# An encoder layer with RWKV-7 time mixing: the chain step on the full array, products that cross between token halves, and projections by halves

## The chip, the cores and the metric

The kernel runs on one core of a Trainium2 chip. The metric is the device time of one execution in microseconds (us). Three runs of the kernel before took 1292.1, 1293.94 and 1299.46 us, median 1293.94.

## The reference

One layer of a streaming encoder works on 576 tokens: 64 that continue a running stream and 512 of a new one. The model is 1024 wide. With h the normalised input, one wide projection feeds three parts, and a gated feed-forward follows:

```python
h = rms_norm(x, g_pre_mix); p = h @ w_in     # r, k, v, three low-rank inputs | u, v of the gMLP | two gates
# time mixing: 16 heads of 64; per token, per head, with decay w, a = -kk, b = kk * a_rate:
sa = einsum('bhvk,bhk->bhv', S, a)
S  = S * w + sa[..., None] * b[:, :, None, :] + v[..., None] * k[:, :, None, :]
y  = einsum('bhvk,bhk->bhv', S, r)
o_a = (group_norm(y) + bonus) * g
o_b = u * (tril(w_spatial) @ layer_norm(v) + bias)            # per chunk of 128 tokens
m = sigmoid(gate_a) * (o_a @ w_proj_a) + sigmoid(gate_b) * (o_b @ w_proj_b)
x = x + rms_norm(m @ w_o); x = x + rms_norm((silu(f @ w_gate) * (f @ w_up)) @ w_down)   # f = rms_norm(x)
```

`r`, `k` and `v` are first mixed with the token before them (token shift). All is fp32. Outputs are the layer's output, the last shifted rows, the final states of both streams and the normalised gMLP rows.

## The kernel before, in words

*Layout.* Activations stand transposed, 128 channels on the partitions and T = 576 tokens along a row (64 of the running stream first), in eight tiles. `HALF` is 288 tokens. A weight block of 128 output columns is one DMA of 512 KB (`wraw`) and is split into a high part `whi` (ScalarE, L289) and a low part `wlo` (GpSimd, two pieces, L292) of the type fp32r; the input likewise into `h0h..h7h` and `h0l..h7l`. A product of a block is then three fp32r products for each of eight k tiles and each token half (`mm`): 48 instructions of 288 columns, `pj` in the profile.

*PSUM.* Eight banks of 512 columns: two tiles of two banks for projections (`ps2`; a projection lies across both banks, columns 224 to 799), three single banks for small products (`ps1`), one for the chain (`ps1c`).

*Time mixing.* The 16 heads are worked as eight pairs (two heads of 64 on the 128 partitions), the tokens as nine chunks of 64. For each pair:

- `elementwise`: decay and rates (`z` products), sums over heads (`n`), the scaled operands `AR` (a and r) and `BK` (b and k); inner products of 64 x 64 within a chunk (`am`), masked into `AB` and `AK`; transposes of b, a, k, v into by-token tiles `Bt`, `At`, `Kt`, `Vt` (`tb`, `tr`, `tv`); `WV`; and the bonus (`bo`).
- `inverse`: the unit triangular 64 x 64 matrix of each chunk and head is inverted: 16 x 16 blocks go through DRAM (`d_inv`) onto 80 partitions, are inverted by 30 VectorE operations (`X`, `Xt`), come back, and are put together by products `m1`, `m2`, `mp`, `mu` into `IT`. `IT` times `Bt` and times the second half of `AB` are the `d` products; `e` are the transition terms (`At` with the result), `c` the constant terms; `y` the part of the output that needs no state.
- `chain`: the state goes from chunk to chunk: `pc` is the transition matrix times the state, VectorE adds the constant term `C` (L916). Chunk 0 is the running stream, chunks 1 to 8 the new one. `py` adds the state's part to `y`.
- `finish`: group norm, transposes back (`to`), gate (`g`).

By-token tiles hold five places of 128 tokens, starting at tokens 0, 128, 256, 384 and 448 (`START`); a place has two halves of 64 partitions (`HR`), so each chunk lies in one half. A product of 64 x 64 uses one of four tiles of TensorE's array: the input's half of partitions by the output's.

*What sets the order.* TensorE's order is written by a planner (`Weave`), when the program is built: streams of small products, each step with an event or a planned latency (`LAT`) before it, are woven into the projections; whenever no stream is ready, the next piece of a projection follows (`project`, one k tile and one half a piece). The planner's clock `clk.now` advances by an estimate for each product. `F0` and `FILL` say how many blocks of gates and u are put between the pairs. The other engines' orders come from the framework's scheduler. In both versions every engine works through its own order and waits on semaphores.

*After the pairs* come the gMLP projections (`gv`), both output projections (`pa`, `pb`), `w_o` (`po`), the feed-forward (`fp`, `fg`) and `w_down` (`po`).

## Time and profile before

| | us |
|---|---|
| median of three runs | 1293.94 |
| the profiled execution, its own time | 1290.25 |
| its span, first to last instruction | 1288.2 |
| of it, TensorE busy | 1218.9 |
| first 60 us, TensorE busy | 44.9 |
| 60 to 630 (the eight pairs and gMLP projections), TensorE busy | 537.0 |
| 630 to 697 (layer norm, first output products), TensorE busy | 59.3 |
| 697 to the end, TensorE busy | 577.7 |

In a row of the timeline the first number is the start, the second the time to the end of the last of its instructions, both in us. Products overlap, so the difference of two starts tells what one costs in a sequence; "busy" is the union of their modelled spans. `PE` is TensorE, `DVE` VectorE, `ACT` ScalarE, `POOL` GpSimd, `SP` the queue that issues DMAs. A row of waits gives the total, the number and the longest. The mean granted TensorE clock of this execution is 0.977 of full speed.

### The profile page before, as it was taken

The numbers are of one execution on the slowest core, as the hardware profiler recorded it, in microseconds if no ns is written. First come the engines' busy times: TensorE is split into PE (matmuls) and PEld (weight loads), VectorE is DVE, ScalarE is ACT, GpSimd is POOL, SyncE is SP. The second block draws the span as 40 slices with busy tenths as digits, with TensorE's granted clock in tenths as the row PEclk, the third lists the DMA queues.
The fourth block names the chain that finished last, engine by engine and source line by source line (L and its number), as shares of the span: only waits on it lengthen the run. The fifth ranks groups of instructions, "written<-read, shape, count | busy, mean of one in ns | idle before, by whom it ended". The sixth has DMA issues, their size and how long they took to land.

```text
span 1288.2 us, 30705 instructions
## 1 busy us (share of the span) xinstructions
PE 1218.9 (95%) x13402; PEld 1171.4 (91%) x13402; DVE 561.4 (44%) x1001; ACT 454.9 (35%) x800; POOL 632.0 (49%) x491
## 2 busy tenths in 40 slices
PE   7799999999999889899989999989999999999997
PEld 6798898888889888889979999989999999999997
DVE  5864645554554636562481443274333333310013
ACT  5634352535253343433332223453222222222220
POOL 6564463442444444431484544356656565644342
PEclk8899999899899999999999999989999999999998
DMA  5222132222131322222535454232222222252222
GB/s 177 79 84 74 47 90 64 69 57 87 41 104 52 89 69 49 81 73 79 168 124 154 136 177 128 69 114 82 94 82 82 83 83 83 82 164 74 84 81 74
DMA packets 68406, 118.61 MB, mean 92 GB/s; under 512 B 30832, under 2 KB 36208, under 8 KB 68272
## 3 DMA queue, kind: packets, MB, share of 16 engines
q1 hardware_dynamic: 68128, 116.58, 30.0%
q8 instruction: 105, 1.72, 0.6%
q14 instruction: 29, 0.24, 0.1%
q10 hardware_dynamic: 144, 0.07, 0.0%
HBM read 100.35 MB, written 16.28 MB: 91 GB/s over the span
## 4 chain that ended last, share of the span: by engine, by line
PE 71%; DVE 13%; ACT 4%; issue 4%; DMA 4%; POOL 2%; SPq 2%; DVEq 0%; ACTq 0%; POOLq 0%
PE fg L273 20%; PE po L273 14%; PE pj L273 13%; PE pb L273 4%; PE pa L273 3%; PE gv L273 3%; DVE Xt L794 2%; DVE X L797 2%; PE am L273 2%; PE y L273 2%; PE d L273 1%; SPq L802 1%; PE fp L273 1%; PE z L273 1%; POOL wlo L292 1%
## 5 line engine op out<-in xcount | busy, mean ns | idle before, releaser
L292 POOL TENSOR_TENSOR wlo<-raw,whi 128x512 fp32r<-128x512 f32 (+1 forms) x288 | 407.3, 1436 | 358.8 <-ACT whi L289 342.4
L289 ACT ACTIVATE whi<-raw 128x1024 fp32r<-128x1024 f32 x144 | 149.8, 1044 | 282.0 <-PE fg L273 172.8
L1179 DVE TENSOR_TENSOR rs<-rs,nsq 128x288 f32<-128x288 f32 (+2 forms) x12 | 9.2, 768 | 104.6 <-ACT nsq L1178 104.6
L1247 DVE TENSOR_TENSOR ft<-ft,fg 128x288 f32<-128x288 f32 x40 | 16.4, 451 | 67.1 <-PE fg L273 65.5
L1241 DVE TENSOR_TENSOR fg<-fg,rs 128x288 f32<-128x288 f32 x40 | 16.5, 453 | 62.3 <-PE fg L273 62.2
L710 POOL TENSOR_TENSOR BK<-BK,EL 128x576 f32<-128x576 f32 x16 | 18.4, 1169 | 49.8 <-PE am L273 45.8
L794 DVE TENSOR_TENSOR Xt<-X,M 80x15 f32<-80x15 f32 (+7 forms) x120 | 35.2, 293 | 8.1 <-DMA M<-d_inv 4.9
L1244 DVE SCALAR_TENSOR_TENSOR ft<-ft,fg 128x576 f32<-128x576 f32 (+1 forms) x24 | 28.9, 1206 | 18.7 <-ACT ft L1243 18.7
L643 POOL TENSOR_TENSOR aq<-aq,k 128x576 f32<-128x576 f32 x8 | 11.8, 1479 | 50.9 <-DVE k L465 49.6
L797 DVE TENSOR_TENSOR X<-X,Xt 80x15 f32<-80x15 f32 (+7 forms) x120 | 35.0, 292 | 3.6
L805 DVE STREAM_TRANSPOSE IT<-IV 128x640 f32<-128x640 f32 x16 | 13.5, 844 | 52.9 <-DMA IV<-d_inv 32.1
L1245 POOL TENSOR_TENSOR ft<-ft,rs 128x576 f32<-128x576 f32 (+1 forms) x24 | 31.8, 1325 | 7.3 <-DVE ft L1244 7.3
L273 PE MATMUL pj<-h4l,whi 128*128 128x288 f32 x92 | 28.6, 311 | 5.5 <-DVE h4l L342 5.5
L273 PE MATMUL am<-AR,BK 64*64 64x128 f32 x640 | 28.5, 284 | 3.4 <-DVE AR L866 1.8
L916 DVE TENSOR_TENSOR S<-pc,C 128x64 f32<-128x64 f32 x48 | 10.7, 222 | 48.3 <-PE pc L273 48.0
L273 PE MATMUL pj<-h0h,whi 128*128 128x288 f32 x92 | 28.7, 312 | 2.7 <-ACT s L431 1.4
L273 PE MATMUL pj<-h0h,wlo 128*128 128x288 f32 x92 | 27.6, 300 | 3.7 <-POOL wlo L292 3.7
L273 PE MATMUL pj<-h5h,whi 128*128 128x288 f32 x92 | 30.3, 329 | 0.0
L273 PE MATMUL pj<-h4h,whi 128*128 128x288 f32 x92 | 29.8, 324 | 0.0
L273 PE MATMUL pj<-h6h,whi 128*128 128x288 f32 x92 | 29.7, 323 | 0.0
L273 PE MATMUL pj<-h3h,whi 128*128 128x288 f32 x92 | 29.3, 319 | 0.0
L273 PE MATMUL pj<-h2h,whi 128*128 128x288 f32 x92 | 29.2, 318 | 0.0
(1239 smaller groups left out, 4331.3 us busy)
## 6 DMA issues: line engine op xcount, KB each, us to landing
raw<-in_w_in SPq DMA_DIRECT2D x50, 512.0 KB, 3.7
raw<-in_w_gate SPq DMA_DIRECT2D x22, 512.0 KB, 3.6
raw<-in_w_up SPq DMA_DIRECT2D x22, 512.0 KB, 3.6
raw<-in_w_down SPq DMA_DIRECT2D x16, 512.0 KB, 3.5
raw<-in_w_gv SPq DMA_DIRECT2D x8, 512.0 KB, 3.7
raw<-in_w_proj_a SPq DMA_DIRECT2D x8, 512.0 KB, 3.7
raw<-in_w_proj_b SPq DMA_DIRECT2D x8, 512.0 KB, 3.5
raw<-in_w_o SPq DMA_DIRECT2D x8, 512.0 KB, 3.5
```

What stands on the lines that cost most here:

```text
L273: return pe.matmul(out, lhsT, rhs, **kw)
L289: keep(act.activation(hi[:, :cols], raw[:, :cols], ACT.Copy))
L292: keep(pool.tensor_tensor(lo[:, c0:c1], raw[:, c0:c1], f(hi[:, c0:c1]), ALU.subtract))
L710: pool.tensor_tensor(by_chunk(BK[:, x, :]), by_chunk(BK[:, x, :]), EL[:, :, 64:65].broadcast_to([P, NCH, 64]), ALU.mult)
L794: ins = dve.tensor_tensor(t3, X[:, 0:r, s:s + 1].broadcast_to([NU, r, w]), M[:, s:s + 1, s + 1:SB].broadcast_to([NU, r, w]), ALU.mult)
L797: dve.tensor_tensor(X[:, 0:r, s + 1:SB], X[:, 0:r, s + 1:SB], t3, ALU.add)
L802: sp.dma_start(IV[r0_:r0_ + SB, :, SB * b:SB * b + SB], di[1, h, b].rearrange("u s t -> s u t"))
L805: turn = lambda: dve.transpose(IT.rearrange("p c t -> p (c t)"), IV.rearrange("p c t -> p (c t)"))
L1241: keep(dve.tensor_tensor(g[:, HS[h]], pg, rs2[:, HS[h]], ALU.mult))
L1244: keep(dve.scalar_tensor_tensor(t[:, ts], t[:, ts], 1.0, g[:, ts], ALU.add, ALU.mult))
L1245: pool.tensor_tensor(t[:, ts], t[:, ts], rs2[:, ts], ALU.mult)
L1247: dve.tensor_tensor(t[:, HS[h]], t[:, HS[h]], pu, ALU.mult)
```

## The change

- *Chain step.* A new tile `TD` holds, for each chunk, a 128 x 128 matrix with the two heads' transition matrices on its diagonal (cleared once). VectorE writes the two blocks from `e`, each head's half by itself. `pc` is then one product on the full array where two 64 x 64 products were.
- *Crossing products.* A second placement, `START2` = 0, 128, 192, 320, 448, holds `AB` and the by-token b, now columns 128 to 191 of `AB` (`Bt` is gone). `d` reads in this placement, writes in the first, and does both operands in one product of 128 columns; `y` reads in the first and writes in the second, and so does the transposition back. The order (`CROSS`) goes round the four tiles.
- *Larger runs.* `d`, `e` and `c` are one run each without planned latencies between the thirds of `d`; `e` waits for the event `values` and the chain of the pair before; the inner products come in two runs where three were; `y` in one where two were.
- *Projections.* Each token half has a bank of its own and is done for all eight k tiles before the other (`project`; evacuation by halves, `Shifted`, `spill`). Three banks for projections, four for small products, one for the chain.
- *Planner.* 0.12 us for a change of the tile's rows, other costs of small products, new latencies.

```diff
...
-    "M": 5.5, "U": 18.5, "m1": 1.8, "m2": 1.7, "mp": 3.3, "mu": 2.0, "d0": 2.2, "d": 0.5, "e0": 1.5, "e1": 0.4, "y0": 1.0,
-    "ch0": 3.0, "S": 1.6, "y": 0.5, "gn1": 4.0, "gn2": 6.0, "to": 3.5, "to1": 0.45, "g": 1.8,
+    "M": 5.5, "U": 20.0, "m1": 2.3, "m2": 2.4, "mp": 3.3, "mu": 2.0, "d0": 2.2, "e0": 2.3, "y0": 3.5,
+    "ch0": 2.6, "S": 1.5, "y": 0.5, "gn1": 4.0, "gn2": 6.0, "to": 3.5, "to1": 0.45, "g": 1.8,
...
-    nb = {"d": 2, "a": 3}
+    nb = {"a": 4}
...
-    ps2 = lambda name: psum.tile([P, 1024], F32, tag="d", bufs=nb["d"], name=name)
+    psd = lambda name: psum.tile([P, 512], F32, tag="d", bufs=3, name=name)
...
+        if rows != clk.rows:
+            clk.now += 0.12
+            clk.rows = rows
...
-            ps = ps2("pj")
-            for k in range(KD):
-                for h in range(2):
-                    mm(ps, ws, hh, hl, k, KD, halves=(h,))
+            held = []
+            for h in range(2):
+                ps = psd("pj")[:, 0:HALF]
+                for k in range(KD):
+                    mm({h: ps}, ws, hh, hl, k, KD, halves=(h,))
                     yield
-            while after is not None and after not in clk.events:
-                yield True
-            done(ps)
+                held.append((h, ps))
+                while h == 1 and after is not None and after not in clk.events:
+                    yield True
+                while held and (after is None or after in clk.events):
+                    done(*held.pop(0))
...
+    class Shifted:
+
+
+        def __init__(self, blk, tag, tp=None, scale=False):
+            self.blk, self.tag, self.tp, self.scale = blk, tag, tp, scale
+
+        def __call__(self, h, ps):
+            blk, hs = self.blk, HS[h]
+            if h == 0:
+                tp = ep if self.tp is None else self.tp
+                self.o = tp.tile([P, T], F32, tag=self.tag, name=self.tag)
+                self.q = tp.tile([P, T + 1], F32, tag="q", name="q")
+            o, q = self.o, self.q
+            if self.scale:
                 dve.tensor_tensor(o[:, hs], ps, rs0[:, hs], ALU.mult)
...
+                ps = o[:, hs]
+            e = (TS, HALF)[h]
+            act.activation(shc[:, blk, h:h + 1], ps[:, e - 1:e], ACT.Copy)
+            act.activation(q[:, hs.start + 1:hs.stop + 1], ps, ACT.Copy, scale=V("mu", blk))
+            if h == 0:
+                act.activation(q[:, 0:TS + 1:TS], first[:, blk, :], ACT.Copy)
+            with tc.high_priority(HPO):
+                dve.scalar_tensor_tensor(o[:, hs], ps, omm[:, blk:blk + 1], q[:, hs], ALU.mult, ALU.add)
+            return o
...
+        for h in range(4):
+            if h == 2:
+                wr = wblock(I["w_in"][BLK_R])
...
+            for k in range(2 if h == 0 else 0, KD):
+                mm(ps, w, uh, ul, k, KD, halves=(h % 2,))
+            if h == 3:
                 clk.prepare()
...
+            act.activation(kr[-1][:, HS[h % 2]], ps[0], ACT.Copy)
...
+    START, START2 = [min(j * P, T - P) for j in range(5)], [0, 128, 192, 320, 448]
+    PLACES, PLACES2 = [[(st[j] // 64 + half_, j, half_) for j in range(5) for half_ in range(2)] for st in (START, START2)]
     CHUNKS = [(c, j, half_) for c, j, half_ in PLACES if (j, half_) != (4, 0)]
     PLACE = {c: (j, half_) for c, j, half_ in CHUNKS}
+    PLACE2 = {c: (j, half_) for c, j, half_ in PLACES2 if (j, half_) != (2, 0)}
+
+    CROSS = [(c, c // 4) for i in range(4) for c in ((i, 4 + i) if i % 2 == 0 else (4 + i, i))] + [(8, 2)]
...
+        pm = banks()
+        for c, j, half_ in PLACES2[:8]:
+            for h, rows in enumerate(HR):
+                inner(pm[h][:, j], HR[half_], rows, 0, c)
+        pn = banks()
+        for c, j, half_ in PLACES2[8:]:
             for x in range(2):
                 for h, rows in enumerate(HR):
-                    inner(pm[h][:, x], HR[half_], rows, x, c)
+                    inner(pn[h][:, x], HR[half_], rows, x, c)
         for h in range(2):
...
+            dve.tensor_tensor(AB[:, 0:4, h, 0:P], pm[h], rmul[:, 0:4, h, :], ALU.mult)
+        for h in range(2):
+            dve.tensor_tensor(AB[:, 4, h, 0:P], pn[h][:, 0], rmul[:, 4, h, :], ALU.mult)
...
-        for i, (dst, src) in enumerate(((Bt, BK[:, 0, :]), (At, AR[:, 0, :]), (Kt, BK[:, 1, :]))):
+        for i, (dst, src) in enumerate(((AB, BK[:, 0, :]), (At, AR[:, 0, :]), (Kt, BK[:, 1, :]))):
             pt = ps1("tb").rearrange("p (j v) -> p j v", v=P)
             for j in range(5):
-                mtrans(pt[:, j] if j < 4 else rest[:, i], src[:, START[j]:START[j] + P], ident)
+                t0 = (START, START2)[i == 0][j]
...
+                    dve.tensor_tensor(dst.rearrange("p j h t -> p (j h) t")[:, u, P:], ps.rearrange("p j (h v) -> p (j h) v", v=HD), rn[:, u].unsqueeze(2).broadcast_to([P, 2 * (j1 - j0), HD]), ALU.mult)
...
-        Bt, At, Kt, Vt, AR, AK, WV = (E[n] for n in ("Bt", "At", "Kt", "Vt", "AR", "AK", "WV"))
-        Bu = Bt.rearrange("p j (h v) -> p (j h) v", v=HD)
-        for u0, u1 in ((0, 4), (4, 8), (8, 10)):
-            pp = ps1("d").rearrange("p (u t) -> p u t", t=P)
-            for u in range(u0, u1):
-                for rows in HR:
-                    mmul(pp[rows, u - u0, 0:64], IT[rows, u, :], Bu[rows, u, :], start=True, stop=True)
-                for rows in HR:
-                    mmul(pp[rows, u - u0, 64:P], IT[rows, u, :], U[rows, u, 64:P], start=True, stop=True)
-            act.activation(U[:, u0:u1], pp[:, 0:u1 - u0], ACT.Copy)
-            yield LAT["d"]
-        yield LAT["e0"]
+        At, Kt, Vt, AR, AK, WV = (E[n] for n in ("At", "Kt", "Vt", "AR", "AK", "WV"))
+        pp = [ps1("d").rearrange("p (u t) -> p u t", t=P) for _ in range(3)]
+        for c, b in CROSS:
+            (j2, half2), (j, half_) = PLACE2[c], PLACE[c]
+            for h in range(2):
+                mmul(pp[b][HR[half_], 2 * (j % 2) + h], IT[HR[half2], 2 * j2 + h, :], AB[HR[half2], j2, h, 64:192], start=True, stop=True)
+        for b, rows, j0, j1 in ((0, slice(0, P), 0, 2), (1, slice(0, P), 2, 4), (2, HR[1], 4, 5)):
+            act.activation(AB[rows, j0:j1, :, 0:P].rearrange("p j h t -> p (j h) t"), pp[b][rows, 0:2 * (j1 - j0)], ACT.Copy)
+        yield (("values", hp_), LAT["e0"])
+        if hp_ > 0:
+            yield (("chain", hp_ - 1), 0.0)
+
 
         pe_ = [ps1("e").rearrange("p (j a t) -> p j a t", a=2, t=64) for _ in range(2)]
...
+        for n in range(2):
+            for c, j, half_ in CHUNKS:
+                for h in range(2):
+                    w, x = (Kt[HR[half_], j, HR[h]], Vt[HR[half_], j, HR[h]]) if n == 0 else (AB[HR[half_], j, h, 64:P], WV[HR[half_], 2 * j + h, :])
+                    mmul(pq[half_][HR[h], j * HD:(j + 1) * HD], w, x, start=n == 0 and j == 0, stop=n == 1, skip_group_check=True)
+        pe8 = pq[1][:, 5 * HD:5 * HD + P].rearrange("p (j a t) -> p j a t", a=2, t=64)
+        for h in range(2):
+            step(pe8[:, 0], 4, 1, h, start=False, skip_group_check=True)
...
+        parts = [(pe_[0], slice(0, 8, 2)), (pe_[1], slice(1, 8, 2)), (pe8, slice(8, 9))]
+        for ps, cs in parts:
+            for rows in HR:
+                dve.tensor_tensor(TD[rows, cs, rows], ps[rows, :, 1, :], by_place[rows, cs, 0, :], ALU.add)
+            dve.tensor_tensor(by_place[:, cs, 1, :], ps[:, :, 0, :], by_place[:, cs, 1, :], ALU.add)
         for half_ in range(2):
...
+            n = 4 + half_
+            act.activation(C[:, half_, 0:n], pq[half_][:, 0:n * HD].rearrange("p (j v) -> p j v", v=HD), ACT.Copy)
         clk.signal("inv", hp_)
         yield LAT["y0"]
         Y = rp2.tile([P, 5, P], F32, tag="Y", bufs=2, name="Y")
...
-                for c, j, half_ in PLACES[2 * j0:2 * j1]:
-                    for h in range(2):
-                        rows, u = HR[half_], 2 * j + h
-                        w, x = (AK[rows, j, h, 64:P], Vt[rows, j, HR[h]]) if n == 0 else (AB[rows, j, h, 64:P], WV[rows, u, :])
-                        mmul(py[rows, u - 2 * j0], w, x, start=n == 0 and (j, h) == (j0, 0), stop=n == 1, skip_group_check=True)
...
+        py = [ps1("y").rearrange("p (u v) -> p u v", v=HD) for _ in range(3)]
+        order = [x for c, _ in CROSS for x in ([(c, *PLACE2[c])] + ([(3, 2, 0)] if c == 3 else []))]
+        for n in range(2):
+            begun = set()
+            for c, j2, half2 in order:
+                b, (j, half_) = j2 // 2, PLACE[c]
+                rows = HR[half_]
+                for h in range(2):
+                    w, x = (AK[rows, j, h, 64:P], Vt[rows, j, HR[h]]) if n == 0 else (AB[rows, j, h, 0:64], WV[rows, 2 * j + h, :])
+                    mmul(py[b][HR[half2], 2 * (j2 % 2) + h], w, x, start=n == 0 and (b, half2) not in begun, stop=n == 1, skip_group_check=True)
+                    begun.add((b, half2))
...
-        cols = lambda c: slice(c * 64, (c + 1) * 64)
         for n, cs in enumerate([(2, 0)] + [(c,) for c in range(3, NCH)]):
             pc = ps1c("pc").rearrange("p (i v) -> p i v", v=HD)
             for i, c in enumerate(cs):
-                for rows in HR:
-                    mmul(pc[rows, i], AR[rows, 0, cols(c)], state(c)[rows], start=i == 0, stop=True, skip_group_check=True)
+                mmul(pc[:, i], TD[:, c, :], state(c), start=True, stop=True)
...
```

More of the change, by code (lines that the diff above doesn't have):

```diff
@@ L143, in __init__ @@
     def __init__(self):
-        self.now = 0.0
+        self.now, self.rows = 0.0, P
         self.events = {}
@@ L271, in mmul @@
         else:
-            clk.now += max(n / 1200, 0.02)
+            clk.now += n / 2000 if rows == 64 else 0.037 if rows == 32 else 0.02
         return pe.matmul(out, lhsT, rhs, **kw)
@@ L556, in layer @@
     dve.tensor_tensor(dar[0:64], xw[64:128], f(dar[64:128]), ALU.subtract)
-    xg = shifted(BLK_DG, "v", list(zip(pf[1], HS)), tp=xp)
+    take = Shifted(BLK_DG, "v", xp, True)
+    xg = [take(h, pf[1][h]) for h in range(2)][1]
     tg = xp.tile([P, T], F32, name="tg")
```

192 lines of the change are left out of this document (74 added, 118 removed).

## The prediction

> **What bounds the kernel now.** I read the stage table first, then TensorE's timeline at single runs of small products, then TensorE's waits, then the instruction order of both kernels.
>
> ```profile
> span 1288.2 us, 30705 instructions
> 60.00:630.00 570.00, 537.00 (x8352) 496.47 (x8352) 290.98 (x609) 227.10 (x461) 238.84 (x186) 0.98 0.25 70
> 697.00:1288.20 591.20, 577.67 (x4332) 573.49 (x4330) 185.41 (x296) 168.46 (x249) 310.04 (x234) 0.99 0.33 101
> 740.52 50.77 PE pb L273 x384
> ```
>
> The last row is from the chain of waits: 384 products of 288 columns without a break in 50.77 us, 0.132 us each, the pace of a projection too. The columns of the stage rows are length, busy time of TensorE, of its weight load, of VectorE, ScalarE and GpSimd, granted clock, DMA share and GB/s. The change lies in the first 60 us and in 60 to 630, where all eight head pairs are worked; after 697 the program is the same. In the pair stage TensorE is busy 537 of 570 us, VectorE 291, ScalarE 227, GpSimd 239. So the stage ends when TensorE has issued its list, and two things matter: how long the list is, and where TensorE waits inside it.
>
> A busy share does not tell what an instruction costs there, since the small products overlap. I take the cost of a run of small products from starts: from the last projection before it to the second projection after it, less two projections at 0.132.
>
> ```profile
> 208.76 0.29 PE L273 MATMUL pj<-h1h,wlo 128*128 128x288 f32 x1
> 208.98 0.33 PE L273 MATMUL pc<-S,AR 64*64 64x64 f32 x4
> ...
> 209.49 0.29 PE L273 MATMUL pj<-h2l,whi 128*128 128x288 f32 x1
> 186.53 0.29 PE L273 MATMUL pj<-h0h,wlo 128*128 128x288 f32 x1
> 186.76 0.33 PE L273 MATMUL d<-Bt,IT 64*64 64x64 f32 x4
> ...
> 188.07 0.29 PE L273 MATMUL pj<-h1l,whi 128*128 128x288 f32 x1
> 201.38 0.29 PE L273 MATMUL pj<-h5h,wlo 128*128 128x288 f32 x1
> 201.60 1.20 PE L273 MATMUL y<-Vt,AK 64*64 64x64 f32 x32
> 202.58 1.15 PE L273 MATMUL y<-WV,AB 64*64 64x64 f32 x32
> ...
> 203.90 0.30 PE L273 MATMUL pj<-h5l,whi 128*128 128x288 f32 x1
> 130.17 0.29 PE L273 MATMUL pj<-h2h,wlo 128*128 128x288 f32 x1
> 130.39 1.10 PE L273 MATMUL e<-AB,At 64*64 64x128 f32 x32
> ...
> 131.66 0.29 PE L273 MATMUL pj<-h3l,whi 128*128 128x288 f32 x1
> ```
>
> Each program instruction on plain fp32 shows as two passes. One chain step (pc, 4 passes): 0.73 - 0.26 = 0.47 us. One third of the d products (16 products, 32 passes, of which the first group of four is shown): 1.54 - 0.26 = 1.28. y: 64 passes, 2.26. pc, d and y use only the two tiles whose input and output halves agree, so they are 2, 16 and 32 passes deep. 1.28 - 0.47 over 14 passes gives 0.058 us for a 64-column pass; what is left, 0.35 us, is paid by every run of small products however short. Check on y: 0.35 + 32 x 0.058 = 2.21 against 2.26. The e run goes over all four tiles, 8 deep: (1.23 - 0.35) / 8 = 0.11 us for a 128-column pass.
>
> So the changeover is the larger part of a chain step, and two of the four tiles stand empty in d and y.
>
> **The change, part by part.** On TensorE, around the second pair's products with the inverses, the chain kernel's order was this before (d: products with the inverse, am: inner products of the next pair, e and c: terms of the chain):
>
> ```order
> L273 MATMUL d<-Bt,IT 64x64 x2
> L273 MATMUL d<-AB,IT 64x64 x2
> L273 MATMUL am<-AR,BK 64x128 x16
> L273 MATMUL pj<-h3h,whi 128x288
> L273 MATMUL pj<-h3l,whi 128x288
> ```
>
> and is this now, in the same place:
>
> ```order
> L271 MATMUL pj<-h7h,wlo 128x288
> L271 MATMUL d<-AB,IT 64x128 x18
> L271 MATMUL e<-AB,At 64x128 x16
> L271 MATMUL c<-Vt,Kt 64x64 x18
> L271 MATMUL c<-WV,AB 64x64 x18
> L271 MATMUL c<-AB,At 64x128 x2
> L271 MATMUL am<-AR,BK 64x128 x16
> L271 MATMUL pj<-h0h,whi 128x288
> ```
>
> All of d, e and c stand in one run, in every one of the eight pairs; projections between d and e, there before, are gone. At a chain step the order was (pc the step, pj projections):
>
> ```order
> L273 MATMUL pj<-h1h,wlo 128x288
> L273 MATMUL pc<-S,AR 64x64 x2
> L273 MATMUL pj<-h2h,whi 128x288
> L273 MATMUL pj<-h2l,whi 128x288
> L273 MATMUL pj<-h2h,wlo 128x288
> ```
>
> and is
>
> ```order
> L271 MATMUL pj<-h0h,wlo 128x288
> L271 MATMUL pc<-S,TD 128x64
> L271 MATMUL pj<-h1h,whi 128x288
> L271 MATMUL pj<-h1l,whi 128x288
> L271 MATMUL pj<-h1h,wlo 128x288
> ```
>
> The step is one full-array product now. Counted over the whole order, runs of small-tile products fall from 142 to 68.
>
> *Changeovers:* 74 fewer x 0.35 = 25.9 us.
>
> *d:* before 40 passes deep a pair, 40 x 0.058 = 2.32; now 18 products of 128 columns over four tiles, the fullest with three chunks x 2 heads x 2 passes, 12 x 0.11 = 1.31. 8 x 1.01 = 8.1 us.
>
> *y:* 40 deep, 2.32, becomes 24 deep (three chunks x 2 heads x 2 terms x 2 passes on the fullest tile), 24 x 0.058 = 1.39, if four tiles of 64 columns go at once. The py products of before do that:
>
> ```profile
> 220.29 0.29 PE L273 MATMUL pj<-h0h,wlo 128*128 128x288 f32 x1
> ...
> 220.75 0.57 PE L273 MATMUL py<-S,AR 64*64 64x64 f32 x26
> 221.49 0.30 PE L273 MATMUL pj<-h1l,whi 128*128 128x288 f32 x1
> 396.15 0.29 PE L273 MATMUL pj<-h3h,wlo 128*128 128x288 f32 x1
> 396.29 1.17 PE L273 MATMUL n<-cst,q 128*128 128x2 f32 x10
> 397.53 0.29 PE L273 MATMUL pj<-h4l,whi 128*128 128x288 f32 x1
> ```
>
> 40 passes, 10 deep on four tiles, take 1.20 - 0.26 = 0.94 (0.35 + 10 x 0.058 = 0.93). So y saves 8 x 0.93 = 7.4 us.
>
> *Chain:* the trace has no full-array product of 64 fp32 columns; nearest is n, 10 passes in 1.38 - 0.26 = 1.12, 0.112 a pass, no changeover. A pair's eight products cost 8 x 2 x 0.112 = 1.79 against 16 passes of 0.058, 0.93: 8 x 0.86 = 6.9 us more (ends: 4 if half of a pass hides behind a projection; 9 at a projection's 0.13 a pass). Its changeovers are in the 74.
>
> The list is shorter by 25.9 + 8.1 + 7.4 - 6.9 = **34.5 us**.
>
> *Waits that go or stay:*
>
> ```profile
> PE m L273 <- ACT PT L816: 8.5, 5, 2.9
> PE tv L277 <- DVE Y L928: 5.1, 3, 2.1
> PE c L273 <- DVE AR L866: 2.9, 2, 1.7
> PE n L273 <- ACT q L639: 2.1, 1, 2.1
> PE am L273 <- DVE AR L866: 1.8, 3, 0.6
> PE am L273 <- ACT AB L853: 1.4, 1, 1.4
> PE c L273 <- DVE AK L688: 1.4, 2, 0.7
> ```
>
> The tv wait is for a PSUM bank that py holds. Now the small products have four banks for three, and tv stands ahead of py or far from it: 5.1 go. The four c and am waits, 7.5, are bank waits inside merged runs; they go with those runs. The m waits (the inverse) I leave as they are: ends -8.5 and +5.
>
> *Waits that come:*
>
> ```profile
> 187.97 0.58 ACT L853 ACTIVATE AB<-d 128x512 f32<-128x512 f32 x1
> 187.02 1.04 ACT L289 ACTIVATE whi<-raw 128x1024 fp32r<-128x1024 f32 x1
> L866 DVE TENSOR_TENSOR AR<-e,AR x16: 628/680/692, 131.8 to 606.6; 128x512 f32<-128x512 f32 x16
> L883 DVE TENSOR_TENSOR AR<-e,AR x8: 291/292/292, 134.2 to 608.4; 128x128 f32<-128x128 f32 x8
> ```
>
> e reads what ScalarE copies from d's banks, and nothing stands between. The copy takes 0.58 and starts about 0.3 after the last pass (d's first third ends by 187.7); first and second bank are full 4 passes (0.44) before d ends. So 0.3 + 0.58 + 0.1 - 0.44 = 0.55, and 0.15 more for the second copy: 0.7 x 8 = 5.6 us (upper end: a weight cast of 1.04 ahead of the copy each time, 14). Behind e all of TensorE's list waits. In four pairs am follows c at once and needs e's second bank, which six VectorE adds empty; 256 columns lie between the two rows above, 0.42 each: 0.3 + 2.5 - 1.3 (c) = 1.5 x 4 = 6. In four pairs d follows am or nearly so and needs the banks that VectorE empties: about 0.75 x 4 = 3. Waits together: +14.6 - 12.6 = **+2 us**.
>
> *DMAs and the other queues.* The eight stores of AB to DRAM that feed the inverse, on SP, stood behind AK's two evacuations on VectorE (L688, the size of the 0.68 row above) and now wait for AB alone: some 1.3 us earlier, in a step that TensorE's order gives more time anyway; I count nothing (cover: the projections between; without it the m waits above). Loads of weights, stores of gates and GpSimd's casts keep number and size; GpSimd clears TD once, at a place where TensorE works off projections.
>
> *Halves of projections* change neither count nor width. They add ScalarE and VectorE instructions (two where one was), hidden behind TensorE as long as it bounds. They cost at the start, where VectorE makes the input tiles:
>
> ```profile
> 45.66 0.29 PE L273 MATMUL pj<-h4h,whi 128*128 128x288 f32 x1
> 51.45 0.61 PE L273 MATMUL pj<-h4l,whi 128*128 128x288 f32 x1 [5.50 <-DVE h4l L342]
> 49.57 1.82 DVE L342 TENSOR_TENSOR h4l<-xn,h4h 128x576 fp32r<-128x576 f32 x1
> 51.31 1.98 DVE L465 SCALAR_TENSOR_TENSOR v<-v,omm,q 128x576 f32<-128x576 f32 x1
> ```
>
> The first block now needs h4l after 12 products instead of 24, so TensorE stands 12 x 0.13 = 1.6 us earlier. VectorE's order there (h4l: low part of the fifth input tile, v: the gate block's shift) was
>
> ```order
> L566 SCALAR_TENSOR_TENSOR xn<-x_130,vec,rs_216 128x576
> L342 TENSOR_TENSOR h4l<-xn,h4h 128x576
> L465 SCALAR_TENSOR_TENSOR v<-v,omm,q 128x576
> L342 TENSOR_TENSOR h6l<-xn,h6h 128x576
> L560 TENSOR_SCALAR tg<-tg 128x576
> ```
>
> and is
>
> ```order
> L473 SCALAR_TENSOR_TENSOR v<-v,omm,q 128x288
> L570 TENSOR_TENSOR dwr<-tw,dwr 64x576
> L473 SCALAR_TENSOR_TENSOR v<-v,omm,q 128x288
> L332 TENSOR_TENSOR h4l<-xn,h4h 128x576
> L332 TENSOR_TENSOR h6l<-xn,h6h 128x576
> ```
>
> Both halves of v are ahead of h4l, 1.98 us later. Of 3.6 us the n wait on q (2.1, at 62) takes up most, since VectorE's own list to there is hardly longer: **+1.5 us**.
>
> Sum: -34.5 + 2 + 1.5 = -31 us. The profiled execution took 1290.25 us around its span of 1288.2; 1290 - 31 = 1259. The median of the runs is 3.7 above it; I forecast **1261**.
>
> **The rivals.** *The waits stay lower (0.15).* If m waits go too (8.5) and lost clock with them (0.98 over 570 us is 11 us, some half of it), 14 more: 1247. For it: every wait there was in a list that is rewritten. Against: m waits on ScalarE's order, which is no calmer now.
>
> *The merged runs eat it (0.13).* With a weight cast ahead of each copy (+8), e's banks 1 us later in four pairs (+4), and am's alike (+4): 1277. For it: the cast at 187.02 stands just ahead of the copy at 187.97. Against: in the new order no cast stands directly ahead of these copies.
>
> *Four tiles do not go at once (0.07).* In d and y, each bank is now written from both input halves. If such products take turns, d is 18 deep (1.97) and y 40 (2.32): 8 x (0.66 + 0.93) = 13 back, 1274. Against: y of before writes one bank from both halves into different partitions, and its 64 passes in 2.26 are two at a time. The Trainium skill (TensorEngine Tiling (Array Packing), Gotcha 1: PSUM Pressure) says that different row tiles cannot access the same PSUM bank simultaneously; by it this rival would hold, and the trace's y speaks against it.
>
> *Another bound (0.05).* The pair's chain through the inverse sets the pace, TensorE stands wherever it got shorter: no change, 1290. Against: the new order leaves 27 projections between the inverse's second and third step, as before, and 15 for 18 before the fourth.
>
> *Slower (0.05).* TensorE's clock is halved after some waits:
>
> ```profile
> 310.20:313.50 3.30, 3.27 (x90) 3.24 (x91) 2.05 (x4) 1.45 (x5) 0.64 (x1) 0.50 0.50 139
> 359.10:363.00 3.90, 3.90 (x58) 3.67 (x59) 3.80 (x13) 1.87 (x5) 0.47 (x1) 1.00 0.11 38
> ```
>
> After the 2.9 us wait for PT it ran at 0.50; after the 2.1 us wait of tv at 1.00.  If each of the sixteen new waits brought two windows of 3.4 us at half clock, 3.4 lost each, that is 54: 1313. From ten of them on the gain is gone. Against: they are 0.7 to 1.7 long. The Trainium skill (TensorE: Matmul & The Clock Gate, Part 1) re-throttles only after an idle window of about 3.4 us; by it none would, though 2.9 did here.
>
> **How the numbers follow.** Forecast 0.55, the rivals 0.45 as given. Its own range is 1252 to 1271. I take 1244 to 1281: from the lower waits to past the merged runs; the bound cases lie outside. This kernel's runs tell changes over 0.5% (6.5 us) from none. Faster: 0.55 + 0.15 + 0.13 + 0.07, less 0.05 for merged runs that eat more than I priced (0.03 to the same, 0.02 to slower), 0.85; same 0.05 + 0.03 = 0.08; slower 0.05 + 0.02 = 0.07.
>
> **What would show it.** Right: the pair stage about 540 us; isolated pc near 0.22 us between projections 0.13 apart; d near 1.3 and y near 1.4 deep; a ScalarE wait of 0.5 to 1 us ahead of e in each pair. Wrong: d or y as long as before (tiles take turns), e waiting over 1.5 us, more time at half clock, or a longer start than 3 us.

## The result, and the profile after

The changed kernel takes 1274.22 us (median of four runs, 1272.39 to 1278.05); the kernel before, beside it, 1293.02. The ratio is 0.985, with a 95% interval of 0.981 to 0.989. The profiled execution took 1273.24 us around a span of 1271.5, 17.0 less than the one before.

The stage table of the changed kernel (columns as in the prediction):

```profile
60.00:630.00 570.00, 529.67 (x8015) 504.22 (x8014) 329.63 (x703) 250.10 (x557) 253.86 (x197) 0.96 0.27 80
630.00:697.00 67.00, 59.83 (x438) 58.91 (x438) 24.78 (x37) 15.78 (x20) 37.88 (x29) 0.95 0.48 141
```

In the same 570 us TensorE is busy 7.3 us less than before, although it gets further in the program, and its granted clock is 0.96 where it was 0.98. VectorE is busy 39 us more, ScalarE 23. So the list of TensorE's work did get shorter, and TensorE spends part of what it saved standing, and part at half clock.

TensorE's timeline of the changed kernel at a chain step and at y:

```profile
150.60 0.29 PE L271 MATMUL pj<-h0h,wlo 128*128 128x288 f32 x1
150.73 0.33 PE L271 MATMUL pc<-S,TD 128*128 128x64 f32 x2
150.87 0.38 PE L271 MATMUL pj<-h1h,whi 128*128 128x288 f32 x1
151.08 0.30 PE L271 MATMUL pj<-h1l,whi 128*128 128x288 f32 x1
...
204.10 0.29 PE L271 MATMUL pj<-h4h,wlo 128*128 128x288 f32 x1
204.33 0.85 PE L271 MATMUL y<-Vt,AK 64*64 64x64 f32 x34
...
205.15 0.91 PE L271 MATMUL y<-WV,AB 64*64 64x64 f32 x34
205.99 0.43 PE L271 MATMUL pc<-S,TD 128*128 128x64 f32 x2
```

The step costs 151.08 - 150.60 - 0.26 = 0.22 us, as forecast (0.47 before). From the last projection to the chain step behind it y takes 205.99 - 204.10 = 1.89; less the projection's 0.13 that is 1.76, against 0.35 + 1.39 forecast. Both prices hold.

At the merged run of d, e and c, with ScalarE's copy of d's banks:

```profile
391.56 1.60 PE L271 MATMUL d<-AB,IT 64*64 64x128 f32 x36
...
392.77 1.49 ACT L882 ACTIVATE AB<-d 128x512 f32<-128x512 f32 x3 [2.31 <-PE d L271]
...
393.91 1.10 PE L271 MATMUL e<-AB,At 64*64 64x128 f32 x32 [0.74 <-ACT AB L882]
```

TensorE's waits in the changed kernel (total, number, longest), between 60 and 640 us:

```profile
PE n L271 <- ACT q L664: 6.9, 3, 2.8
PE e L271 <- ACT AB L882: 5.5, 8, 0.7
PE mp L271 <- DVE IT L836: 3.9, 2, 2.3
PE tr L275 <- DVE AB L757: 3.5, 2, 2.1
PE gv L271 <- POOL wlo L290: 3.0, 2, 2.7
PE pc L271 <- DVE So L946: 2.7, 2, 2.0
PE am L271 <- DVE AR L909: 2.4, 3, 0.8
PE tv L275 <- DVE Y L958: 2.3, 1, 2.3
PE pc L271 <- DVE S L946: 1.5, 2, 1.2
...
PE m L271 <- ACT PT L847: 1.1, 2, 0.6
```

The m waits for ScalarE's PT (8.5 before) are down to 1.1. The e wait is there eight times, as forecast. n, mp, tr and pc wait for ScalarE and VectorE more than before. In the kernel before n waited 2.1 us for q, tr 0.2 us, and pc

```profile
PE pc L273 <- DVE S L916: 0.8, 1, 0.8
```

To put the whole together I charge every instruction of TensorE its price (as in the prediction: 0.132 a projection, 0.058 and 0.11 a pass on the fullest tile, 0.111 a full-array pass; 0.34 where the prediction had 0.35 for a run of small products). What an interval takes beyond that is clock, up to half of its overlap with a half-clock stretch; else wait. "Pairs" is 60 to 640 us; a wait is counted where it is over 0.25 us, what is smaller stands by itself. Some 14 us of each span lie ahead of TensorE's first and behind its last instruction. Sums of the two profiled executions in us:

| | before | after | difference | forecast |
|---|---|---|---|---|
| list | 1169.7 | 1135.3 | -34.4 | -34.5 |
| pairs: waits | 42.4 | 49.4 | +7.0 | +2 |
| pairs: smaller excess | 8.0 | 9.6 | +1.6 | 0 |
| pairs: lost clock | 12.6 | 20.3 | +7.7 | 0 |
| first 60 us, all three | 16.9 | 18.4 | +1.5 | +1.5 |
| after 640: waits and excess | 19.6 | 17.4 | -2.2 | 0 |
| after 640: lost clock | 5.0 | 6.8 | +1.8 | 0 |
| sum | | | -17.0 | -31 |

The list agrees with the forecast by its making, since it is the same counts at nearly the same prices. What tests the prices is the smaller excess, where a wrong price would show (it grew by 1.6), and the chain step and y above. The 14 us between forecast and result are clock (9.5) and waits with the smaller excess (6.6 more in the pairs than forecast, 2.2 fewer later).

How a wait costs clock: three stretches of 3.41 us of the changed kernel, from n's second wait on (113.2 to 115.2):

```profile
112.34:115.75 3.41, 1.39 (x12) 1.15 (x10) 1.01 (x2) 3.18 (x8) 0.19 (x1) 1.00 0.51 153
115.75:119.16 3.41, 3.41 (x93) 3.36 (x93) 1.99 (x4) 2.70 (x7) 2.69 (x2) 0.50 0.02 5
119.16:122.58 3.42, 3.42 (x16) 3.42 (x16) 2.41 (x2) 0.10 (x2) 2.93 (x2) 0.50 0.00 0
```

TensorE is busy 1.39 of 3.41 us, and the next two stretches of that length are granted half. I call these stretches windows. All half-clock stretches of both kernels, but for the one at the very end, begin and end on multiples of 3.413 us from each other.

### The profile page after: what moved, and what is told of

Read it like the earlier page. It is cut to its first block, busy times and chain, and to the rows that moved or that the text cites. A ratio compares the mean times of both kernels' runs of the same rounds, so it can differ in the third digit from the quotient of the medians.

```text
span 1271.5 us, 29927 instructions
## 1 busy us (share of the span) xinstructions
PE 1195.4 (94%) x12922; PEld 1162.5 (91%) x12922; DVE 583.3 (46%) x1077; ACT 466.2 (37%) x887; POOL 630.5 (50%) x492
## 4 chain that ended last, share of the span: by engine, by line
PE 68%; DVE 15%; ACT 5%; POOL 4%; issue 4%; DMA 3%; SPq 1%; DVEq 0%; POOLq 0%; ACTq 0%
PE fg L271 20%; PE po L271 14%; PE pj L271 11%; PE pb L271 4%; PE pa L271 4%; PE gv L271 3%; POOL wlo L290 2%; DVE X L828 2%; PE am L271 1%; DVE Xt L825 1%; PE fp L271 1%; SPq L833 1%; PE z L271 1%; PE pc L271 1%; DVE L L650 1%
## 5 line engine op out<-in xcount | busy, mean ns | idle before, releaser
L828 DVE TENSOR_TENSOR X<-X,Xt 80x15 f32<-80x15 f32 (+7 forms) x120 | 42.4, 353 | 3.4
L976 POOL TENSOR_TENSOR gm<-gm,mhalf 128x10 f32<-128x10 f32 x8 | 16.2, 2023 | 42.8 <-DVE gm L975 42.8
L271 PE MATMUL pj<-h1h,whi 128*128 128x288 f32 x92 | 29.6, 321 | 0.0
L271 PE MATMUL pj<-h7h,whi 128*128 128x288 f32 x92 | 29.3, 319 | 0.0
```

Of the source, the lines that this page charges most:

```text
L271: return pe.matmul(out, lhsT, rhs, **kw)
L828: dve.tensor_tensor(X[:, 0:r, s + 1:SB], X[:, 0:r, s + 1:SB], t3, ALU.add)
L976: pool.tensor_tensor(m, m, mhalf, ALU.pow)
```

## The experiments

My theory after the result: the list is right, and the rest is waits that ScalarE and VectorE cause because TensorE now reaches n, mp and the chain steps earlier, with lost clock behind them. Rivals: the full-array step itself brings the waits; the order that the planner made is at fault, not the step; a pace that other engines set.

**The changed kernel again, as a control.**

> The changed kernel again, as the control for the three that run beside it: about 1274 us, granted clock 0.96 to 0.97 in the pair stage, the same waits of n for ScalarE's q at 64, 113 and 240 us. The windows of half clock should stand behind the same waits; if they stand elsewhere, the loss of clock is chance of the execution and not a property of the order.

Measured: 1275.05 us (1271.79 to 1278.66), ratio 0.987 (0.984 to 0.990). Waits in the pairs 52.6, lost clock there 16.8 (49.4 and 20.3 in the first execution). So two executions of one kernel differ by 3.2 us in waits and 3.5 in clock, and differences of that size between other traces say nothing. The n waits stand where they stood, but a half-clock stretch of 6.8 us behind the run at 128 us is missing. The large waits belong to the order; part of the lost clock is chance of the execution.

**The chain step alone undone.**

```diff
-            for rows in HR:
-                dve.tensor_tensor(TD[rows, cs, rows], ps[rows, :, 1, :], by_place[rows, cs, 0, :], ALU.add)
+            dve.tensor_tensor(by_place[:, cs, 0, :], ps[:, :, 1, :], by_place[:, cs, 0, :], ALU.add)
...
-                mmul(pc[:, i], TD[:, c, :], state(c), start=True, stop=True)
+                for rows in HR:
+                    mmul(pc[rows, i], AR[rows, 0, c * 64:(c + 1) * 64], state(c)[rows], start=i == 0, stop=True, skip_group_check=True)
```

> The chain step alone is put back to two 64 x 64 products on the transition part of AR; TD is gone, the rest of the change stays. List theory (a run of small products costs 0.34 us and its passes, a full-array pass 0.111): runs of small products rise from 68 to 112 (+15.0 us), their passes by 7.5 us, and 128 full-array passes go (-14.2): +8.3 us, 1282 to 1283. Rival, the chain step is nearly all of the gain: +17, 1291. Rival, its shorter list only bought waits: no change, 1274.

Measured: 1260.79 us (1258.62 to 1263.18), ratio 0.976 (0.974 to 0.979), 14 us *faster* than the control beside it. None of the three forecasts had this. The list is 8.2 us longer, as computed (1143.5); the waits in the pairs fall by 9.5, lost clock there by 3.0, waits after 640 by 6.2. Undoing the step also changes the planner's charge for it, and with that TensorE's whole order. So step and order had to be taken apart.

**The square of step and order.** Both kernels keep the other's order to the instruction:

```diff
+                if clk.rows != 64:
+                    clk.now += 0.12
+                    clk.rows = 64
+                clk.now += 2 * 64 / 2000
-                mmul(pc[:, i], TD[:, c, :], state(c), start=True, stop=True)
+                pe.matmul(pc[:, i], TD[:, c, :], state(c), start=True, stop=True)
```

> The chain step stays one full-array product, but the planner is charged for it what it charged for two 64 x 64 products (0.30 us a step with the changes of rows, where 0.21 is charged in the changed kernel), so that TensorE's order is exactly that of c1_chain_two. Order theory (the wider step is right, but its order leaves the other engines too little time): list 8.2 us shorter than in c1_chain_two at equal waits, 1252 to 1254. Step theory (the full-array step or its six VectorE adds cost what c1 gained): 1272 to 1275. Pace theory (the other engines set the pace in either order, TensorE's shorter list turns into waits): 1260.

> The other half of the square: the chain step is two 64 x 64 products as in c1_chain_two, in exactly the order of the changed kernel. Order theory: the list is 8.2 us longer than in the changed kernel at equal waits, 1280 to 1283. Step theory: as c1_chain_two, 1261. Pace theory: the longer list fills the waits, 1273 to 1275.

Medians in us, ratio to the kernel before beside them with its interval, and from the traces the list and the waits in the pairs:

| | order of the changed kernel | order of c1_chain_two |
|---|---|---|
| one full-array product | 1275.05; 0.987 (0.984 to 0.990); list 1135.3, waits 52.6 | 1262.98; 0.975 (0.972 to 0.979); 1136.3, 52.7 |
| two 64 x 64 products | 1270.71; 0.981 (0.978 to 0.984); list 1143.4, waits 44.2 | 1260.79; 0.976 (0.974 to 0.979); 1143.5, 43.1 |

Down a column, eight us of list buy nothing: the waits grow by 8.4 and 9.6. That is nearest to the pace theory, which had 1260 and 1273 to 1275 and is missed by 2 to 3 us both times. Across a row the order moves the time by 1.2% with one product and 0.5% with two, at equal list and equal waits in the pairs. Order theory and step theory both fall in their sizes. With the full-array product the order's gain is, in the traces, lost clock (start, pairs and end together 30.0 in the control, 23.5 here) and waits after 640 (13.3 against 8.3).

Where part of these waits comes from under the full-array step shows in VectorE's groups and the am waits, in the same order of TensorE. With the full-array product (c5_full_order_of_two):

```profile
L908 DVE TENSOR_TENSOR TD<-e,AR 64x256 f32<-64x256 f32 x32 | 13.4, 419 | 20.1 <-PE e L271 19.9
L909 DVE TENSOR_TENSOR AR<-e,AR 128x256 f32<-128x256 f32 x16 | 6.8, 425 | 0.2
PE am L271 <- DVE AR L909: 3.2, 4, 0.8
```

With two products (c1_chain_two):

```profile
L905 DVE TENSOR_TENSOR AR<-e,AR 128x256 f32<-128x256 f32 x16 | 6.7, 418 | 20.1 <-PE e L271 20.1
L906 DVE TENSOR_TENSOR AR<-e,AR 128x256 f32<-128x256 f32 x16 | 6.6, 413 | 0.0
PE am L271 <- DVE AR L906: 0.6, 3, 0.2
```

The two heads' blocks of TD are written by two instructions of 64 partitions, 0.419 us each, where one of 128 partitions takes 0.418. e's two banks are emptied in six adds instead of four, 0.84 us later, and in four pairs am stands behind them: the excess of these four runs is 0.9 to 1.1 us larger each, 4.2 in all (2.6 of them in the am rows above). That is under half of the 9.6; the rest is spread over mp, mu and the chain steps. Whether the shorter list brings it, or VectorE's added work there too, is not separated.

**A cover for ScalarE's copy.** The half of c that needs nothing of d is moved ahead of e:

```diff
+        cterm(0, (0,))
         yield (("values", hp_), LAT["e0"])
         pe_ = [ps1("e").rearrange("p (j a t) -> p j a t", a=2, t=64) for _ in range(2)]
...
+        cterm(0, (1,))
+        cterm(1, (0, 1))
```

> Eight products of c that need nothing of d (Kt with Vt, first halves; 0.46 us of passes) are put between d and e, so that the copy of d's banks has cover; number of runs and passes are the same. If e's wait is what it looks like (0.75 us, ScalarE's copy), it falls to about 0.3 in each pair: -3.6 us, and the half-clock stretch behind the run at 128 us goes (3.4 us at the least): 1267 to 1270. Rival, the wait comes back at the am products behind e and c (they wait for VectorE emptying e's bank, which now starts later): four pairs give back 0.4 each, 1272. Rival, the wait does not shrink: 1274.

Measured: 1274.97 us (1273.19 to 1276.05), the control's 1275.05. The wait hardly shrank, as the last rival had it. The moved products in TensorE's timeline:

```profile
392.14 1.28 PE L271 MATMUL d<-AB,IT 64*64 64x128 f32 x33
393.15 0.27 PE L271 MATMUL c<-Vt,Kt 64*64 64x64 f32 x2
...
393.49 0.34 PE L271 MATMUL c<-Vt,Kt 64*64 64x64 f32 x6
394.49 1.10 PE L271 MATMUL e<-AB,At 64*64 64x128 f32 x32 [0.65 <-ACT AB L883]
```

The moved products ran inside d's last passes, on tiles that d had left empty, and 0.65 us behind them is idle, 0.74 before. Behind e nothing got shorter, since c's length is that of the other half, which has five chunks against four. I had moved work that was not on the fullest tile; the whole run takes 4.97 us between its projections in both kernels. The theory of e's wait was not tested by this.

**n planned later**, alone and with two products:

```diff
-    "z0": 5.4, "z": 0.85, "n2": 4.9,
+    "z0": 5.4, "z": 0.85, "n2": 7.0,
...
-    "n2@0": 1.4,
+    "n2@0": 4.4,
```

> Only two planned latencies change: the sums over heads (n) come 2.1 us of projections later after k in each pair (3.0 in the first). Clock theory (a wait that leaves TensorE idle for about half of a 3.4 us window costs the next one or two windows at half clock): the waits of n for q (6.9 us) go and with them the half-clock stretches at 68, 116 and 242 us (17 us at half clock, 8.5 lost): 1259. Waits-only theory: -6.9, 1267. Rival, the waits only move to the next steps of the same chain (inner products, inverse): 1272 to 1276.

> c1_chain_two with the sums over heads (n) planned 2.1 us later (3.0 in the first pair), as in c4_n_later. There this gave 6 us. If the n waits (6.2 us in c1_chain_two) and the half-clock stretches behind them (68 and 116 us, 5 us lost) go here too: 1252 to 1256. Rival, the waits move to the inverse as they partly did in c4_n_later (0.5 us of wait left over in sum): 1258 to 1261.

> c7_two_n_later with two planned latencies more: the inverse's third step (mp) 1.7 us of projections later, the first pair's n 2.0 later. If these waits (mp 6.4 us, n 3.5) are filled with projections and the half-clock stretches at 65 and 185 us go: 1247 to 1250. Rival, the chain through the inverse is only pushed back and the waits return at d, e and the chain steps: 1255 to 1259.

Alone: 1268.66 us (1265.42 to 1272.12), ratio 0.981 (0.979 to 0.984), 6.4 under the control. That is near the 1267 of waits alone and not the 1259 of the clock theory: the half-clock stretch at 68 us was to go and stands at 67.13, two windows long where it was one. What became of the waits, in the kernel with n later:

```profile
PE mp L271 <- DVE rn L677: 4.5, 3, 2.6
PE n L271 <- ACT q L664: 3.1, 1, 3.1
```

n's own waits fell from 6.8 to 3.1 us, but rn on VectorE comes with n and now stands ahead of the inverse's transposition, so mp waits (6.8 us for rn and IT together, 5.3 in the control). In the profiled executions waits in the pairs fall by 2.0 only, less than the control's own spread; this execution was the slowest of its four, so the accounting does not settle where the median's 6.4 came from.

With two products: 1256.88 us (1256.45 to 1262.01), ratio 0.972 (0.968 to 0.975), between its forecast (1252 to 1256) and the rival's 1258 to 1261, and the best of all: faster than the kernel before by 2.8%, and its interval lies clear of the changed kernel's. From c1_chain_two it is not told apart (0.974 to 0.979).

With mp later too: 1267.07 us (1265.79 to 1267.92), a clear miss; I had forecast 1247 to 1250. The stage rows of the pairs, first c7_two_n_later, then this one:

```profile
60.00:640.00 580.00, 546.90 (x8267) 512.48 (x8266) 326.86 (x704) 258.73 (x566) 273.87 (x212) 0.98 0.29 83
```

```profile
60.00:640.00 580.00, 545.13 (x8207) 510.90 (x8206) 313.89 (x696) 250.97 (x560) 258.26 (x202) 0.96 0.27 79
```

Waits in the pairs fell by 2.1 (43.0 to 40.9), but lost clock grew by 9.7 (12.3 to 22.0): hardly fewer waits, and in worse places.

**The same list in other orders.** One number of the planner is changed, 0.12 to 0.10 and to 0.14:

```diff
-            clk.now += 0.12
+            clk.now += 0.10
```

> The changed kernel with one number of the planner other: a change of the tile's rows is charged 0.10 us where 0.12 was. Every instruction and the number of runs stay, only their order moves a little (runs of small products stand one or two projections elsewhere). If the time is set by the length of the list and the mean slack, 1273 to 1277. If where single waits fall decides (clock windows, the end of the pair stage), as the square of chain step and order suggests, it moves by 4 to 12 us, in either direction.

> As c10_row_010 with 0.14: the same two theories, 1273 to 1277 or 4 to 12 us away. A trend (0.10 slower and 0.14 faster, or the other way round) would say that the slack given to the small products counts; two moves without a trend say that it is where single waits fall.

Measured: 1268.78 us (1267.67 to 1277.79), ratio 0.983 (0.979 to 0.988), and 1266.44 us (1264.53 to 1269.06), ratio 0.980 (0.976 to 0.984). The control has 0.987 (0.984 to 0.990). Both medians are 6 to 9 us lower, so there is no trend. The interval of 0.14 lies below the control's but overlaps the first measurement's (0.981 to 0.989); that of 0.10 overlaps both. List and waits in the pairs are the control's (1135.3 and 1135.4; 52.6 in all three). What fell in both traces is the waits after 640 (13.3 in the control; 9.9 and 9.6). The largest of them, in the changed kernel:

```profile
647.64 2.57 POOL L1102 TENSOR_TENSOR s<-s,s 128x512 f32<-128x512 f32 x2
...
650.18 3.40 POOL L290 TENSOR_TENSOR wlo<-raw,whi 128x512 fp32r<-128x512 f32 x2
...
651.94 0.61 PE L271 MATMUL pj<-h0h,wlo 128*128 128x288 f32 x1 [4.87 <-POOL wlo L290]
```

On GpSimd a weight's low part stands behind a product of the layer norm, and TensorE waits 4.9 us. In these two orders that wait is 2.9 and 1.8, in c5_full_order_of_two 2.4. It goes with the order at the end of the last pair; why GpSimd's two pieces of work stand this way round in one order and not in another I have not followed.

**Round the four tiles or one by one.**

```diff
-    CROSS = [(c, c // 4) for i in range(4) for c in ((i, 4 + i) if i % 2 == 0 else (4 + i, i))] + [(8, 2)]
+    CROSS = [(c, c // 4) for c in (0, 2, 4, 6, 5, 7, 1, 3, 8)]
```

> d and y go through one tile of the array after the other (0, 2, 4, 6, 5, 7, 1, 3, 8) instead of round the four tiles; the products are the same. If each tile works off its own products behind the others, however they are ordered, y still takes 1.80 us between projections and the time stays at 1275. If a tile's turn has to come in the order of issue, y goes towards its 80 passes of 0.058 (up to 4.9 us) and d towards 36 of 0.11: up to 45 us more, 1285 to 1320.

Measured: 1287.57 us in a single execution, and y in its timeline:

```profile
409.87 0.29 PE L271 MATMUL pj<-h2h,wlo 128*128 128x288 f32 x1
410.09 1.59 PE L271 MATMUL y<-Vt,AK 64*64 64x64 f32 x37
...
411.70 1.55 PE L271 MATMUL y<-WV,AB 64*64 64x64 f32 x37
413.18 0.43 PE L271 MATMUL pc<-S,TD 128*128 128x64 f32 x2
```

y takes 413.18 - 409.87 = 3.31 us where it took 1.89, 1.42 x 8 = 11.4 us for y alone; the merged runs of d, e and c are 0.9 longer in five pairs (5.87 for 4.97 where nothing else is in the run) and 0 to 2.5 longer in the other three. The time grew by 12.5 us in all. The truth lies between the two theories: tiles work side by side, but only over a stretch of the order of issue. Going round them is part of what the crossing products earn.

**What a stall costs.** The computation is whole; 40 stalls are added:

```diff
+        pe.matmul(bank[:, 0:P], ident, ident, start=True, stop=True)
+        act.activation(junk[:, 0:P], bank[:, 0:P], ACT.Copy)
+        for _ in range(len(nstall) % 5):
+            act.activation(junk, junk, ACT.Copy)
+        pe.matmul(bank[:, P:P + 1], ident, junk[:, 0:1], start=True, stop=True)
```

> The changed kernel with 40 stalls put into the feed-forward's projections, where nothing else waits: one small full-array product, ScalarE copies its bank and then copies a tile onto itself 0 to 4 times, a second product needs the result. Stalls of about 0.8 to 3 us, one every 6.5 us of projections. Grid theory (the clock is decided every 3.41 us by how busy TensorE was in that window): half-clock stretches begin only on multiples of 3.41 us from each other, and behind a stall only where one window holds about 1.9 us or more of it (busy share under 0.45); stalls of 1 us bring none, stalls of 2 us bring one in about half of the cases. Length theory: every stall above some length brings one at once, wherever it falls. Total: 1275 and the stalls, about 75 us, and 1.7 to 3.4 us more for each stretch.

Measured: 1408.01 us. TensorE stood 0.43, 1.09, 1.75, 2.41 or 3.07 us, eight times each (but 1.22 for the first of 1.09, and 1.88 for the first of 1.75). Windows, with a stall of 2.41 us in the one from 939.57, one of 3.07 us across those from 949.80 and 953.22, one of 1.75 us in the one from 977.10. The rows begin 0.07 us ahead of the grid itself:

```profile
939.57:942.98 3.41, 1.00 (x9) 0.81 (x7) 0.00 (x0) 2.17 (x4) 2.16 (x2) 1.00 0.47 113
942.98:946.39 3.41, 3.41 (x15) 3.41 (x16) 0.00 (x0) 0.00 (x0) 0.00 (x0) 0.51 0.10 41
946.39:949.80 3.41, 3.41 (x27) 3.41 (x27) 1.64 (x3) 1.75 (x2) 1.52 (x2) 0.99 0.00 0
949.80:953.22 3.42, 1.76 (x14) 1.56 (x12) 0.39 (x1) 1.50 (x3) 1.54 (x1) 1.00 0.24 37
953.22:956.63 3.41, 2.00 (x15) 2.00 (x16) 0.00 (x0) 1.29 (x3) 0.00 (x0) 1.00 0.29 117
956.63:960.04 3.41, 3.41 (x28) 3.41 (x27) 1.89 (x3) 1.67 (x2) 1.58 (x2) 1.00 0.02 5
...
977.10:980.52 3.42, 1.67 (x13) 1.48 (x13) 0.00 (x0) 1.54 (x3) 1.40 (x2) 1.00 0.57 158
980.52:983.93 3.41, 3.41 (x17) 3.41 (x16) 0.82 (x2) 1.29 (x2) 0.32 (x1) 0.51 0.00 0
```

The stall of 3.07 us, cut in two by the grid's edge (1.72 and 1.35; 1.66 and 1.41 by the rows), brought no half clock; those of 2.41 and 1.75, whole in one window, did. Over all 40: every stall of 2.41 us brought it (each had at least 2.33 us in one window), none of 1.09 or 0.43. Those of 1.75 did the four times that they lay whole in one window and not the four times that they were cut; those of 3.07 did the five times that one window held 1.90 us or more and not at 1.60, 1.72 and 1.85. For these stalls the grid theory stands; its point lies at about half a window (1.75 us of idle time, a little lower than the 1.9 that I had taken), with 1.85 as the one exception. Behind these stalls the stretch is one window if that window is itself busy 0.98 or more, two if it is not (0.66 to 0.84, the stall's second piece). Among small products that does not hold: the stretch at 115.75 above is two windows long, though TensorE is busy through the first.

## Why the prediction was right, and where it was wrong

Right in sign and range (1244 to 1281), 13 us off in the number: less than two thirds of the forecast gain came. The sum of -31 would give 1263 from the median of 1293.94; the forecast of 1261 lies between that and the 1259 of the profiled execution.

- *Changeovers, d, y, chain:* -34.5 forecast, -34.4 by the same counts and prices in the traces; what the traces show by themselves is the step at 0.22, y at 1.76 and 68 runs for 142. No run undoes the merged runs, the crossing placement or the halves of projections by itself, so their worth rests on these prices.
- *The start:* +1.5 forecast, +1.5 found, but by luck. The sum had h4l made 1.98 us later and the n wait taking up most of that. h4l was made earlier (from 48.18 us; 49.57 before) and its wait fell from 5.5 us, while new waits of 2.3 us came for two weight parts and h5l, and the n wait behind them grew:

```profile
PE pj L271 <- DVE h4l L332: 3.5, 1, 3.5
```

- *Waits that come:* the kind and place were right. e waits eight times, 5.5 us in all; the run costs 1.05 for it where 0.7 was forecast (4.97 against 0.34 + 3.58 without a wait, the 3.58 being 22 passes of 0.11 and 20 of 0.058). With am behind it is 2.55 in the two pairs where nothing else is in the run, so 1.5 more, as forecast. For d behind am 3 us were forecast and 1.1 came.
- *Waits that go:* the m waits, which the sum leaves as they are, went (8.5 to 1.1), tv by 2.8 instead of 5.1.
- *The step that failed first:* "They add ScalarE and VectorE instructions, hidden behind TensorE as long as it bounds." A busy share of half did not hide a chain that TensorE waits for. n went from 2.1 to 6.9, and mp (3.9), tr (3.5) and pc (4.2) came, for ScalarE and VectorE, where TensorE's new order left them less time than they took. In the square, eight us less of list came with eight to ten more of waits, 4.2 of them behind the step's own adds. How much of the rest is the shorter list, and how much the added instructions of the halves, no run separates.
- *The step that was missing:* the sum had no term for the clock. I had put it into two rivals, at sixteen new waits of 0.7 to 1.7 us. The 9.5 us came mostly behind waits of 2 to 5 us that I had not foreseen (n at 64, 113 and 240 us, a chain step at 325, two weight parts at 613 and 647).
- *The chain step:* priced rightly on TensorE and worth nothing in this kernel: TD costs VectorE two more adds that am waits for, and the rest of the time saved is waited away at places whose cause stays open.
- *The rivals:* four tiles do go at once, if the order goes round them. The Trainium skill (TensorEngine Tiling (Array Packing), Gotcha 1: PSUM Pressure) says that different row tiles cannot use one PSUM bank at the same time. y's 1.76 us for 80 passes of 0.058 into three banks, from both halves of the rows, speaks against it. "Another bound" was given 0.05 as a case of its own; in the square a bound of that kind took the whole gain of one part.

By the traces the number 1274 falls by chance on that of the four-tile rival; its mechanism was not at work.

## What to carry to other kernels

When a statically ordered engine's list gets shorter, do not count on the whole gain (here 17 of 31 us came) and ask of every product that follows a chain over other engines whether that chain gets shorter too; where it does not, the gain is a wait. Undo each part by itself afterwards, and keep the order fixed when you do: here a part that was right by its price was worth nothing, and the order that a planner happened to make was worth 0.5 to 1.2%. Judge a wait by its length *within* a clock window as well as by its sum.

## What the hardware showed that was not expected

- The half-clock stretches lie on a fixed grid of 3.413 us. In the run with stalls every window with 1.88 us or more idle put the next one, or two, at half clock, and so did 1.75 us four times, but not 1.85. The limit is not sharp: in the control a window with 1.90 us idle, behind a wait of tr, did nothing:

```profile
85.55:88.96 3.41, 1.51 (x13) 1.27 (x11) 1.30 (x6) 0.77 (x2) 0.14 (x1) 1.00 0.77 236
88.96:92.38 3.42, 3.24 (x26) 3.24 (x27) 3.14 (x11) 1.40 (x5) 1.15 (x1) 1.00 0.03 13
```

- The Trainium skill (TensorE: Matmul & The Clock Gate, Part 1) names a free-running window of 3413 ns, and the edges here agree with it. Its rule (there under HAM oscillation) is to have no idle gaps over some 3.4 us; that is too mild by these runs, where 1.75 us was enough four times, and 3.07 us did nothing when an edge cut it near the middle.
- So a wait of 2 us costs 2 us, or 1.7 to 3.4 more for one or two windows at half clock, by where the grid lies in that execution (the kernel before has one stretch of three windows, from 241.86): two executions of the changed kernel with the same order lost 20.3 and 16.8 us in the pairs.
- Products on four tiles run side by side only as far as the order of issue mixes them: y's 80 passes take 1.89 us round the tiles and 3.31 one tile after the other.
- Not settled is how small products count. In the changed kernel the window of the run at 128 us was busy 2.17 of 3.41 us by the records, more than half, and the next was granted half (0.50). The control has the same products, but the grid cuts them elsewhere; its windows there are busy 2.48 to 3.35 and none behind them is at half clock. Nor is busy time alone the rule: the changed kernel's window from 177.20 was busy 2.98 of 3.41, and the next was granted half. The window of the run at 128 us:

```profile
129.41:132.82 3.41, 2.17 (x44) 1.49 (x42) 2.39 (x7) 0.95 (x3) 1.92 (x2) 1.00 0.24 99
```

- A VectorE add of 256 columns from PSUM takes 0.42 us on 64 partitions and on 128: splitting one by halves of the partitions doubles it.
